# A two-layer trunk on one NeuronCore: seven block products for a pair of up-projection tiles in place of eight

## The chip, the cores and the metric

The kernel runs on one core of a Trainium2 chip. The metric is the device time of one execution in microseconds (us), as the median of several runs. The engines are TensorE (PE in the profile, PEld for its weight loads), VectorE (DVE), ScalarE (ACT), GpSimd (POOL) and SyncE (SP, which issues the DMAs).

## The reference

The reference is a trunk of two layers on 512 tokens of width 1024, with 16 learned meta tokens ahead, 528 in all. The first layer's mixer is a sparse attention over selected keys, the second's a differential attention. Each layer ends with a gated ConvFFN, and the change is in these two ConvFFNs:

```python
def conv_ffn(h, w_up, conv_w, conv_b, w_down):
    Tp = h.shape[1]
    u = h @ w_up                                   # 1024 -> 2 * 2816
    up = jnp.pad(u, ((0, 0), (CONV_W - 1, 0), (0, 0)))
    c = conv_b + sum(up[:, j:j + Tp] * conv_w[j] for j in range(CONV_W))
    gate, val = jnp.split(c, 2, axis=-1)
    return (jax.nn.silu(gate) * val) @ w_down      # 2816 -> 1024
...
    h = h + conv_ffn(rms_norm(h, ln_ffn_g[i]), w_up[i], conv_w[i], conv_b[i], w_down[i])
```

Everything is float32.

## The kernel before

Activations lie transposed: features on the partitions, tokens on the free axis. The state `h` is 8 tiles of 128 features by 528 tokens. For a matmul each float32 operand is split into a high part in fp32r (a cast on ScalarE) and a low part (the difference, on VectorE or GpSimd), and a product is the sum of three matmuls: high by high, high by low, low by high. A matmul has one weight block of 128 by 128 and moves the columns of one half of the tokens (272 and 256 in the first layer; 260 and 256 in the second, which leaves out 12 meta tokens; down-projections of the second move 512 at once).

The weights go through `Weights`: a DMA on SP brings a tile of up to 8 blocks of K by 128 outputs into `raw` (512 KB, three buffers), `split` makes `hi` and `lo` (L111, L113; three buffers each), `take` gives the next pair to TensorE, `done` frees it, and `pump` loads and splits as far as buffers are free, in the order in which the tiles were planned.

A ConvFFN (`ffn`, L1050) normalises `h` and then walks over f = 0 to 21. For each f it computes two up tiles, gate (e = 0) and value (e = 1), in `lin` (L227): 8 blocks of K, two halves of the tokens, three matmuls each, 48 matmuls into a PSUM tile of two banks. `evac` (L1061) applies the convolution: a ScalarE pass with scale and bias (L1065) and two VectorE instructions that add the shifted columns (L1068), all reading PSUM. After the value tile ScalarE takes SiLU (L1073), VectorE the product (L1074), and the activation is split into `ah` and `al` (L1077, L1078). After f = 6, 12, 17 and at the end, `down` (L1120) multiplies the 6, 6, 5 and 5 activations gathered since with the down weights: 8 output tiles one after the other, and VectorE adds each from PSUM to `h` (L1116).

PSUM has eight banks: two tiles of two banks (tag `sp`: up tiles and every other down tile) and four single ones (tag `one`). Instructions are traced in the program's order; the framework then orders each engine's queue by priorities and a time model, and sets the semaphores.

Of the kernel before, what the change touches and what calls it, by code (L numbers as in the profile page):

```python
# [9 lines left out]
F32 = mybir.dt.float32  # L10
# [4 lines left out]
DRAM = bass.MemoryType.DRAM  # L15

# [50 lines left out]
class Weights:  # L67
# [4 lines left out]
    RAW = 3  # L72
    RING = 3

    def __init__(self, nc, pool, par):
        self.nc, self.pool, self.par = nc, pool, par
        self.units, self.loads, self.raw, self.out = [], [], {}, {}
        self.loaded = self.scaled = self.ready = self.taken = self.freed = 0
        self.held = 0

    def add(self, src, n=8, m=128, g=None, lo="v", fold=None):
        self.units.append((n, m, lo))
        self.loads.append((src, n, m, g, fold))

    def load(self):
        src, n, m, g, fold = self.loads[self.loaded]
        raw = self.pool.tile([128, 8, 128], F32, tag="raw", name="raw", bufs=self.RAW)
        dst = raw[:, :n, :m]
        self.nc.sync.dma_start(dst if fold is None else dst.rearrange("p (a k) c -> p a k c", a=fold), src)
        self.raw[self.loaded] = raw  # L90
        self.loaded += 1

    def scale(self):
        src, n, m, g, fold = self.loads[self.scaled]
        if g is not None:
            r = self.raw[self.scaled][:, :n, :m]
            self.nc.gpsimd.tensor_tensor(r, r, self.par[:, g:g + n, None].to_broadcast([128, n, m]), op=OP.mult)  # L97
        self.scaled += 1

    def split(self):  # L100
        nc = self.nc
        n, m, lo = self.units[self.ready]
        raw = self.raw.pop(self.ready)
        self.freed += 1
        r = raw[:, :n, :m]
        hi = self.pool.tile([128, 8, 128], F32R, tag="hi", name="hi", bufs=self.RING)
        lt = self.pool.tile([128, 8, 128], F32R, tag="lo", name="lo", bufs=self.RING)
        if lo == "pp":
            nc.gpsimd.tensor_scalar(hi[:, :n, :m], r, 1.0, 1.0, op0=OP.mult, op1=OP.mult)
        else:  # L110
            nc.scalar.copy(hi[:, :n, :m], r)  # L111
        eng = nc.vector if lo == "v" else nc.gpsimd
        eng.tensor_tensor(lt[:, :n, :m], r, hi[:, :n, :m].bitcast(F32), op=OP.subtract)  # L113
        self.out[self.ready] = (hi, lt)
        self.held += 1
        self.ready += 1

    def can_split(self):
        return self.ready < self.scaled and self.held < self.RING

    def pump(self, stop=None):
        while stop is None or self.ready < stop:
            if self.loaded < min(len(self.loads), self.freed + self.RAW):
                self.load()
            elif self.scaled < self.loaded:
                self.scale()
            elif self.can_split():
                self.split()
            else:
                return  # L130
# [10 lines left out]
    def done(self):  # L141
        self.held -= 1
# [7 lines left out]
class Trunk:  # L150
# [88 lines left out]

    def halves(self, name):  # L240
# [11 lines left out]
    def setup(self):  # L252
# [15 lines left out]
        self.wt = Weights(nc, self.W, par)  # L268
# [62 lines left out]
    PARTS = ((0, 6), (6, 12), (12, 17), (17, 22))  # L331
    PW = ((0,0),(0,1),(1,0))

    def plan_ffn(self, l):
        wu, wd = self.a["w_up"][l], self.a["w_down"][l]
        for f in range(NF):
# [1311 lines left out]
```

## Time and profile before

| | us |
|---|---|
| Median of 3 runs | 1387.37 |
| Lowest and highest run | 1386.98, 1393.93 |
| The profiled execution, its own time | 1384.77 |
| Its span, first to last instruction | 1383.0 |

The page gives each engine's busy time, the chain of waits that ended last, and the costliest groups of instructions; a matmul's recorded duration is longer than its share of the stream, since matmuls are pipelined, so the rate is read from the distance of events that repeat. In the trace the tiles of f = 0 and 1 of the first ConvFFN are computed around 280 to 306 us.

### The profile page before, as it was taken

What the parts mean: (1) busy time and instruction counts of PE and PEld (TensorE: products, weight loads), DVE (VectorE), ACT (ScalarE), POOL (GpSimd) and SP (SyncE); (2) the same over time, 40 slices, a digit from 0 to 9 for tenths busy, and PEclk for the clock granted to TensorE, in tenths of its full rate; (3) what the DMA queues carried; (4) which work ended last, traced back from release to release, by engine and by line L of the source; (5) the groups of instructions that cost most, each with busy time, mean ns of one, the idle gap of its engine ahead of it and who ended that gap; (6) DMA issues with size and microseconds to landing.
All of it is one profiled execution on the core that took longest, in us unless ns stands there. A gap on an engine that the chain in (4) does not pass through costs nothing.

```text
span 1383.0 us, 25034 instructions
## 1 busy us (share of the span) xinstructions
PE 1324.3 (96%) x10072; PEld 1278.4 (92%) x10072; DVE 852.2 (62%) x1734; ACT 589.3 (43%) x1114; POOL 286.2 (21%) x334
## 2 busy tenths in 40 slices
PE   5999899999999999999799999989899999999998
PEld 4999789899999999999799999989799899899897
DVE  6499977665445445555756767775755445545453
ACT  4453555554224333234435555655544234333231
POOL 3514533400000000002554533444500000000000
PEclk9999989999999999999999989999999999999999
DMA  7412222122332232323223222212222332332422
GB/s 233 118 48 89 84 70 80 61 78 81 88 95 82 85 107 69 106 83 89 73 80 85 79 66 64 72 48 69 77 62 84 93 109 85 88 107 64 121 71 97
DMA packets 46995, 118.98 MB, mean 86 GB/s; under 512 B 5936, under 2 KB 15456, under 8 KB 46880
## 3 DMA queue, kind: packets, MB, share of 16 engines
q1 hardware_dynamic: 46128, 114.57, 27.8%
q0 software_dynamic: 752, 2.82, 0.7%
q8 instruction: 79, 1.29, 0.4%
q14 instruction: 36, 0.29, 0.1%
HBM read 112.46 MB, written 4.91 MB: 85 GB/s over the span
## 4 chain that ended last, share of the span: by engine, by line
PE 84%; DVE 8%; ACT 2%; issue 2%; POOL 2%; DMA 1%; SPq 0%; POOLq 0%; DVEq 0%; ACTq 0%
PE lin L222 56%; PE dn L1105 17%; PE pv L1005 1%; PE stq L567 1%; PE pv L1453 1%; DVE lo L113 1%; PE sa L910 1%; DVE acc L447 1%; ACT hi L111 1%; PE linh L222 1%; DVE xl L517 1%; PE pt L1014 1%; PE stk L557 1%; PE pt L1467 1%; PE sb L1379 1%
## 5 line engine op out<-in xcount | busy, mean ns | idle before, releaser
L222 PE MATMUL lin<-xh,hi 128*128 128x256 f32 (+3 forms) x2208 | 635.0, 289 | 12.7 <-DVE ht L434 7.0
L222 PE MATMUL lin<-xl,hi 128*128 128x256 f32 (+3 forms) x2208 | 634.1, 287 | 2.4 <-POOL xl L517 1.8
L222 PE MATMUL lin<-xh,lo 128*128 128x256 f32 (+3 forms) x2208 | 634.5, 288 | 0.0
L222 PEld LDWEIGHTS lin<-xh,hi 128*128 128x128 f32 (+1 forms) x2208 | 420.6, 191 | 16.3 <-ACT xh L542 5.0
L222 PEld LDWEIGHTS lin<-xl,hi 128*128 128x128 f32 (+1 forms) x2208 | 421.5, 191 | 4.3 <-POOL xl L517 2.2
L222 PEld LDWEIGHTS lin<-xh,lo 128*128 128x128 f32 (+1 forms) x2208 | 421.6, 191 | 0.1
L111 ACT CAST hi<-raw 128x1024 fp32r<-128x1024 f32 (+3 forms) x209 | 199.4, 956 | 332.3 <-PE lin L222 167.0
L113 DVE TENSOR_TENSOR lo<-raw,hi 128x1024 fp32r<-128x1024 f32 (+3 forms) x180 | 201.9, 1123 | 223.1 <-ACT hi L111 222.7
L1105 PE MATMUL dn<-ah,hi 128*128 128x256 f32 (+2 forms) x528 | 142.3, 322 | 0.5 <-DVE ht L1116 0.5
L1105 PE MATMUL dn<-al,hi 128*128 128x256 f32 (+2 forms) x528 | 142.5, 321 | 0.0
L1105 PE MATMUL dn<-ah,lo 128*128 128x256 f32 (+2 forms) x528 | 141.9, 321 | 0.0
L1068 DVE SCALAR_TENSOR_TENSOR c<-lin,par,c 128x512 f32<-128x512 f32 (+2 forms) x172 | 129.7, 755 | 2.9
L1116 DVE TENSOR_TENSOR ht<-dn,ht 128x256 f32<-128x256 f32 (+2 forms) x96 | 46.6, 514 | 116.3 <-PE dn L1105 116.3
L1105 PEld LDWEIGHTS dn<-ah,hi 128*128 128x128 f32 x528 | 88.9, 188 | 9.0 <-DVE ht L1116 0.8
L1105 PEld LDWEIGHTS dn<-ah,lo 128*128 128x128 f32 x528 | 88.9, 188 | 7.8
L1105 PEld LDWEIGHTS dn<-al,hi 128*128 128x128 f32 x528 | 89.0, 188 | 7.4
L447 POOL TENSOR_TENSOR acc<-acc,nsq 128x256 f32<-128x256 f32 (+2 forms) x18 | 16.6, 929 | 378.2 <-PE dn L1105 360.7
L113 POOL TENSOR_TENSOR lo<-raw,hi 128x1024 fp32r<-128x1024 f32 (+1 forms) x31 | 70.3, 2268 | 64.7 <-ACT hi L111 64.3
L1077 ACT CAST ah<-c 128x528 fp32r<-128x528 f32 (+1 forms) x44 | 27.6, 627 | 102.9 <-DVE c L1074 102.9
L1065 ACT ACTIVATE c<-lin,par 128x528 f32<-128x528 f32 (+1 forms) x86 | 67.2, 781 | 0.0
L1073 ACT ACTIVATE c<-c 128x528 f32<-128x528 f32 (+1 forms) x44 | 28.1, 639 | 83.7 <-DVE c L1068 83.7
L97 POOL TENSOR_TENSOR raw<-raw,par 128x1024 f32<-128x1024 f32 x24 | 47.3, 1971 | 69.1 <-DMA raw<-w_kv 34.7
(255 smaller groups left out, 1760.8 us busy)
## 6 DMA issues: line engine op xcount, KB each, us to landing
raw<-w_up SPq DMA_DIRECT2D x88, 512.0 KB, 3.5
raw<-w_down SPq DMA_DIRECT2D x32, 384.0 KB, 3.1
raw<-w_down SPq DMA_DIRECT2D x32, 320.0 KB, 2.9
raw<-w_in SPq DMA_DIRECT2D x16, 512.0 KB, 3.6
raw<-w_kv SPq DMA_DIRECT2D x16, 512.0 KB, 3.7
nb<-nbias SPq DMA_DIRECT2D x16, 264.0 KB, 2.7
raw<-w_o_a SPq DMA_DIRECT2D x8, 512.0 KB, 3.6
raw<-w_q SPq DMA_DIRECT2D x8, 512.0 KB, 3.5
```

The costliest lines, as they stand in the source:

```text
L97: self.nc.gpsimd.tensor_tensor(r, r, self.par[:, g:g + n, None].to_broadcast([128, n, m]), op=OP.mult)
L111: nc.scalar.copy(hi[:, :n, :m], r)
L113: eng.tensor_tensor(lt[:, :n, :m], r, hi[:, :n, :m].bitcast(F32), op=OP.subtract)
L222: i = self.nc.tensor.matmul(o, w[wi][:, kw + k, :m], x[s][xi][:, kx + k, c0:HN[s]], start=(first and p == 0), stop=(last and p == 2))
L447: eng.tensor_tensor(acc, acc, sq[:, :n], op=OP.add)
L517: i = eng.tensor_tensor(xl[:, m, o:o + n], xfs[m][:, :n], xh[:, m, o:o + n].bitcast(F32), op=OP.subtract)
L1065: nc.scalar.activation(t[:, :n], u[:, off + t0:off + T], AF.Identity, bias=b, scale=w2)
L1068: nc.vector.scalar_tensor_tensor(t[:, z:n], u[:, off + t0 + z - d:off + T - d], w, t[:, z:n], op0=OP.mult, op1=OP.add)
L1073: nc.scalar.activation(c[:, :n], c[:, :n], AF.Silu)
L1077: nc.scalar.copy(ah[:, :n], c[:, :n])
L1105: nc.tensor.matmul(part(t, c0, c1, o), w[wi][:, k, :], acts[f][ai][:, c0:c1], start=(first and p == 0), stop=(last and p == 2))
L1116: nc.vector.tensor_tensor(hv, part(t, c0, c1, o), hv, op=OP.add)
```

## The change

For f = 2 to 21 the gate and the value tile of one f are computed together in `up_pair`. The two tiles are taken as a 2 by 2 block matrix: G1, G2 are the gate's blocks of K 0 to 3 and 4 to 7, V1, V2 the value's. The tokens are halved at the middle (264 columns each in the first layer, 258 in the second). In place of 8 block products of 12 matmuls there are 7 (`product`), a scheme of Strassen's kind:

- weight sums S1 = V1 + V2, S2 = S1 - G1, S3 = G1 - V1, S4 = G2 - S2, four VectorE adds of 4 x 128 columns for each pair (`sum`), which are then split like other weights;
- token sums T, once per ConvFFN (`input_sums`): TensorE adds the blocks in PSUM by matmuls with the identity and minus the identity, and ScalarE and VectorE split them; these steps stand between those of the tiles of f = 0 and 1;
- the products accumulate in PSUM in the two-bank tiles `g` and `v`; ScalarE copies the first product from `g` to `v` and the second to SBUF (`p5`), and VectorE adds twice from `v` and `p5` into `g` and `v`.

Per pair the streams hold: in `wt` the gate tile, S12 and S34 (8 blocks each), in a second `Weights` object `ws` with half-size buffers the value's second half (4 blocks) and the down weights. The down groups are now 4, 4, 4, 4 and 6. The first four are computed inside later pairs, one tile per slot: pairs f = 4 to 19 hold a late tile each, f = 5 to 20 a middle one, each in two halves (of 12 matmuls in the first layer, 6 of 512 columns in the second), and VectorE adds it to `h`. The last group (16 to 21) is computed behind the pairs as before.

Over the pairs the queues of TensorE, VectorE and ScalarE hold the program's order (`manual_schedule`); `early` places a cast and `late` the low part by hand, and the pump only loads. The product, the split of the activation and the late tile's add of pair f stand at the start of pair f + 1.

The diff, cut to its core:

```diff
...
+    def sum(self):
+        p, half = divmod(self.summed, 2)
+        g, v = self.pairs[p]
+        kind = ("S12", "S34")[half]
+        assert g["ok"] and v["ok"] and kind not in self.sums, "no weights to sum up"
+        t = self.extra.tile([128, 8, 128], F32, tag=kind, name=kind, bufs=1)
+        gw, vw = g["raw"], v["raw"]
+        add = self.nc.vector.tensor_tensor
+        if half == 0:
+            add(t[:, 0:4], vw[:, 0:4], vw[:, 4:8], op=OP.add)
+            add(t[:, 4:8], t[:, 0:4], gw[:, 0:4], op=OP.subtract)
+            self.s2 = t[:, 4:8]
+        else:
+            add(t[:, 4:8], gw[:, 4:8], self.s2, op=OP.subtract)
+            add(t[:, 0:4], gw[:, 0:4], vw[:, 0:4], op=OP.subtract)
+        for r in (g, v):
...
+        self.sums[kind] = t
+        self.summed += 1
+        self.pump()
...
+    def cast(self):
+        nc = self.nc
+        kind, r, k, n, m, lo = self.units[self.ready + len(self.half)]
+        src = r["raw"] if kind == "raw" else self.sums.pop(kind)
+        src = src[:, k:k + n, :m]
...
+            nc.scalar.copy(hi[:, :n, :m], src)
+        self.half.append((hi, lt, src))
+    def rest(self):
...
+        eng.tensor_tensor(lt[:, :n, :m], src, hi[:, :n, :m].bitcast(F32), op=OP.subtract)
+        if kind == "raw":
+            r["reads"] -= 1
...
-    PARTS = ((0, 6), (6, 12), (12, 17), (17, 22))
-    PW = ((0,0),(0,1),(1,0))
+    PLAIN = 2
+    PARTS = ((0, 4), (4, 8), (8, 12), (12, 16))
+    TAIL = 16
+    PW = ((0, 0), (0, 1), (1, 0))
+    def down_slots(self):
+        late = {f1 + q: (p, 2 * q) for p, (_, f1) in enumerate(self.PARTS) for q in range(4)}
+        return late, {f + 1: (p, m + 1) for f, (p, m) in late.items()}
     def plan_ffn(self, l):
...
-                self.wt.add(wu[f + NF * e], lo=('p' if (f, e) in self.PW else 'v'))
-            for f0, f1 in self.PARTS:
-                if f == (f1 if f1 < NF else NF - 1):
-                    for m in range(KC):
-                        self.wt.add(wd[m][:, f0:f1, :], n=f1 - f0, lo="vv"[m % 2])
+                wt.add(wu[f + NF * e], lo='p' if (f, e) in self.PW else 'v')
+        for f in range(self.PLAIN, NF):
+            g, v = (wt.load_of(wu[f + NF * e]) for e in range(2))
+            wt.unit("raw", g)
+            pair = wt.pair(g, v)
+            wt.unit("S12", pair)
+            wt.unit("S34", pair)
+            for slot in (mid, late):
+                if f in slot:
+                    p, m = slot[f]
+                    f0, f1 = self.PARTS[p]
+                    ws.add(wd[m][:, f0:f1, :], n=4)
+            ws.unit("raw", v, 4, 4)
+        ws.ends.append(len(ws.loads))
+        for m in range(KC):
+            wt.add(wd[m][:, self.TAIL:NF, :], n=NF - self.TAIL, lo="v")
...
+            def input_sums():
...
+                def add(t, k, blocks, first):
+                    for p, (z, b) in enumerate(blocks):
+                        xs, k0, c = B[b]
+                        for e in range(2):
+                            nc.tensor.matmul(t, same[z], xs[2 + e][:, k0 + k, c:c + N],
+                                             start=(first and p == 0 and e == 0), stop=(p == len(blocks) - 1 and e == 1),
+                                             skip_group_check=not first)
+                    self.pe(2 * len(blocks) * mm_cost(N))
+                def split(t, j, k, sign):
+                    hi, lo = (TT[j][z][:, k, :N] for z in range(2))
+                    nc.scalar.mul(hi, t, sign)
+                    if sign > 0:
+                        nc.vector.tensor_tensor(lo, t, hi.bitcast(F32), op=OP.subtract)
+                    else:
+                        nc.vector.scalar_tensor_tensor(lo, t, sign, hi.bitcast(F32), op0=OP.mult, op1=OP.subtract)
...
+                    t = bank()
+                    add(t, k, ((0, (1, 2)), (1, (1, 1))), True)
+                    split(t, 0, k, 1.0)
+                def three(k):
+                    banks[k] = bank()
+                    add(banks[k], k, ((0, (2, 2)), (1, (1, 2))), True)
+                    split(banks[k], 2, k, 1.0)
+                def two(k):
+                    add(banks[k], k, ((0, (1, 1)),), False)
+                    split(banks[k], 1, k, 1.0)
+                def four(k):
+                    add(banks[k], k, ((1, (2, 1)),), False)
+                    split(banks[k], 3, k, -1.0)
+                for fn, k in ((three, 0), (one, 0), (two, 0), (one, 1), (four, 0), (three, 1), (one, 2), (two, 1),
+                              (one, 3), (four, 1), (three, 2), (three, 3), (two, 2), (two, 3), (four, 2), (four, 3)):
+                    fn(k)
+                    yield
+            def product(out, w, wk, xs, xk, c0, first=True):
+                for k in range(4):
+                    for p, (wi, xi) in enumerate(((0, 0), (0, 1), (1, 0))):
+                        nc.tensor.matmul(out, w[wi][:, wk + k, :], xs[xi][:, xk + k, c0:c0 + N],
+                                         start=(first and k == 0 and p == 0), stop=(k == 3 and p == 2), skip_group_check=not first)
+                    self.pe(3 * mm_cost(N))
+                    self.poll()
+            def up_pair(f):
...
+                more = f + 1 < NF
+                n3, ns = wt.taken, ws.taken
+                a, b = ((z.get(f) and down(*z[f])) or iter(()) for z in (at_mid, at_late))
+                g = ps.tile([128, 1024], F32, tag="sp", name="g")
+                g0, g1 = g[:, off + st0:512], g[:, 512:512 + N]
+                for i in range(ns, ns + (f in at_mid) + (f in at_late) + 1):
+                    ws.early(i)
+                before = rest.pop(f - 1, iter(()))
+                next(before, None)
+                while ws.half:
+                    ws.late()
+                G, S12 = wt.take(), wt.take()
+                product(g0, G, 0, x0, 0, st0)
+                v = ps.tile([128, 1024], F32, tag="sp", name="v")
+                v0, v1 = v[:, off + st0:512], v[:, 512:512 + N]
+                nc.scalar.copy(v0, g0)
+                next(before, None)
+                product(g1, S12, 0, TT[0], 0, 0)
+                p5 = fp.tile([128, 264], F32, tag="p", name="p5", bufs=2)[:, :N]
+                nc.scalar.copy(p5, g1)
+                if more:
+                    wt.sum()
+                next(a, None)
+                product(v0, S12, 4, TT[1], 0, 0, False)
+                nc.vector.tensor_tensor(g1, v0, p5, op=OP.add)
+                if more:
+                    wt.sum()
+                product(g0, G, 4, x0, 4, st0, False)
+                wt.done()
+                wt.done()
+                wt.early(n3 + 3)
+                wt.late()
+                wt.early(n3 + 4)
+                next(a, None)
+                next(a, None)
+                if f in at_mid:
+                    ws.done()
+                if f + 1 in at_mid:
+                    ws.early(ws.taken + (f in at_late) + 1)
+                S34 = wt.take()
+                product(v0, S34, 0, TT[2], 0, 0, False)
+                nc.vector.tensor_tensor(v1, v0, p5, op=OP.add)
+                wt.late()
+                ws.late()
+                product(g1, S34, 4, x1, 4, mid - 264, False)
+                wt.done()
+                convolve(g, f, 0, off)
+                wt.early(n3 + 5)
+                wt.late()
+                next(b, None)
+                nc.scalar.activation(conv[0][:, :n], conv[0][:, :n], AF.Silu)
+                A22 = ws.take()
+                product(v0, A22, 0, TT[3], 0, 0, False)
+                convolve(v, f, 1, off)
+                next(b, None)
+                if f in at_late:
+                    ws.done()
+                ws.done()
+                rest[f] = finish_pair(f, conv[0], conv[1], b)
+            def finish_pair(f, c, t, b):
+                nc.vector.tensor_tensor(c[:, :n], c[:, :n], t[:, :n], op=OP.mult)
+                next(b, None)
+                yield
+                split_acts(f, c)
+                yield
...
-            self.run(self.lin_many(x, first[2:], 0))
+            more = input_sums()
+            self.run(self.beside(self.lin_many(x, first[2:], 0), more))
...
+            def down(p, m):
+                f0, f1 = self.PARTS[p]
+                t, w = new(), ws.take()
+                for k in range(f1 - f0):
+                    if k == (f1 - f0) // 2:
+                        yield
+                    block(t, w, f0 + k, k, cols, k == 0, k == f1 - f0 - 1)
+                yield
+                add(t, m, cols, False)
+                yield
...
-            for f in range(1, NF):
+            at_late, at_mid = self.down_slots()
+            with self.tc.issue_after(self.low.ins):
+                wt.sum()
+                wt.sum()
+            for f in range(1, self.PLAIN):
                 for e in range(2):
                     if (f, e) != (1, 0):
-                        self.run(self.lin(x, lambda u, f=f, e=e: evac(u, f, e), start=st0, tag="sp"))
-                for f0, f1 in self.PARTS[:-1]:
-                    if f == f1:
-                        down(f0, f1)
+                        self.run(self.beside(self.lin(x, lambda u, f=f, e=e: evac(u, f, e), start=st0, tag="sp"), more))
+            self.run(more)
+            wt.auto = ws.auto = False
+            with self.tc.manual_schedule(engines=ENGINES):
+                for f in range(self.PLAIN, NF):
+                    up_pair(f)
+                for _ in rest.pop(NF - 1):
+                    pass
+            wt.auto = ws.auto = True
+            wt.pump()
             if l == 0:
                 self.table(AF.Sqrt, conv[0][:, 0:1])
-            down(*self.PARTS[-1])
+            down_last(self.TAIL, NF)
```

## Rows read from the trace of the kernel before

**Rows 1.** Page part 1: busy us (share of the span) xinstructions of each engine.

```profile
...
PE 1324.3 (96%) x10072; PEld 1278.4 (92%) x10072; DVE 852.2 (62%) x1734; ACT 589.3 (43%) x1114; POOL 286.2 (21%) x334
...
```

**Rows 2.** Page part 4, the chain that ended last: share of the span by line.

```profile
...
PE lin L222 56%; PE dn L1105 17%; PE pv L1005 1%; PE stq L567 1%; PE pv L1453 1%; DVE lo L113 1%; PE sa L910 1%; DVE acc L447 1%; ACT hi L111 1%; PE linh L222 1%; DVE xl L517 1%; PE pt L1014 1%; PE stk L557 1%; PE pt L1467 1%; PE sb L1379 1%
...
```

**Rows 3.** Timeline of ScalarE, both ConvFFNs: start us, us, engine, instruction, idle before, releaser.

```profile
...
300.14 0.79 ACT L1065 ACTIVATE c<-lin,par 128x528 f32<-128x528 f32 x1
...
306.02 0.79 ACT L1065 ACTIVATE c<-lin,par 128x528 f32<-128x528 f32 x1
...
1131.45 0.78 ACT L1065 ACTIVATE c<-lin,par 128x512 f32<-128x512 f32 x1
...
1137.15 0.78 ACT L1065 ACTIVATE c<-lin,par 128x512 f32<-128x512 f32 x1
...
```

**Rows 4.** Timeline of VectorE in down-projections of both ConvFFNs.

```profile
...
485.84 0.77 DVE L1116 TENSOR_TENSOR ht<-dn,ht 128x256 f32<-128x256 f32 x2 [2.83 <-PE dn L1105]
...
494.65 0.77 DVE L1116 TENSOR_TENSOR ht<-dn,ht 128x256 f32<-128x256 f32 x2 [2.35 <-PE dn L1105]
...
1094.11 0.69 DVE L1116 TENSOR_TENSOR ht<-dn,ht 128x512 f32<-128x512 f32 x1 [1.56 <-PE dn L1105]
...
1098.29 0.69 DVE L1116 TENSOR_TENSOR ht<-dn,ht 128x512 f32<-128x512 f32 x1 [2.54 <-PE dn L1105]
...
```

**Rows 5.** Lines by form: line, engine, instruction xcount, busy us, mean ns, idle before.

```profile
...
L111 ACT CAST hi<-raw 128x1024 fp32r<-128x1024 f32 x136 | 142.4, 1047 | 193.6 <-PE lin L222 129.7 <-PE dn L1105 56.1 <-POOL tm L889 2.8
...
L1065 ACT ACTIVATE c<-lin,par 128x528 f32<-128x528 f32 x43 | 33.9, 787 | 0.0
...
L1116 DVE TENSOR_TENSOR ht<-dn,ht 128x512 f32<-128x512 f32 x32 | 22.0, 690 | 60.2 <-PE dn L1105 60.2
...
L1074 DVE TENSOR_TENSOR c<-c,c 128x528 f32<-128x528 f32 x22 | 15.6, 708 | 0.7
...
L1116 DVE TENSOR_TENSOR ht<-dn,ht 128x272 f32<-128x272 f32 x32 | 13.7, 430 | 0.0
...
```

**Rows 6.** Timeline of VectorE at the opening of the first ConvFFN.

```profile
...
289.31 1.23 DVE L113 TENSOR_TENSOR lo<-raw,hi 128x1024 fp32r<-128x1024 f32 x1 [5.98 <-ACT hi L111]
...
290.45 0.76 DVE L1068 SCALAR_TENSOR_TENSOR c<-lin,par,c 128x527 f32<-128x527 f32 x1
...
307.29 1.56 DVE L1068 SCALAR_TENSOR_TENSOR c<-lin,par,c 128x527 f32<-128x527 f32 x2
...
```

**Rows 7.** Timeline of all engines, opening of the first ConvFFN.

```profile
...
291.17 0.29 PE L222 MATMUL linh<-xh,hi 128*128 128x272 f32 x1
...
292.57 0.38 ACT L1092 COPY u<-linh 128x272 f32<-128x272 f32 x1
...
293.17 0.36 PE L222 MATMUL lin<-xh,hi 128*128 128x272 f32 x1 [1.46 <-DVE c L1068]
...
```

**Rows 8.** Windows: stretch, us, busy us of each engine, PEclk, DMA share, GB/s.

```profile
...
293.00:305.00 12.00, 11.83 (x97) 11.86 (x98) 9.08 (x13) 6.31 (x8) 0.00 (x0) 1.00 0.49 150
...
305.00:317.00 12.00, 12.00 (x101) 12.00 (x100) 6.94 (x9) 4.95 (x7) 0.00 (x0) 1.00 0.28 89
...
475.00:513.00 38.00, 38.00 (x313) 38.00 (x312) 14.88 (x23) 9.77 (x11) 0.00 (x0) 1.00 0.36 108
...
286.00:294.00 8.00, 6.54 (x53) 6.35 (x52) 4.69 (x6) 5.70 (x8) 0.00 (x0) 1.00 0.26 70
...
661.00:668.00 7.00, 3.35 (x24) 2.83 (x22) 6.68 (x10) 3.75 (x7) 2.01 (x2) 1.00 0.21 73
...
668.00:675.00 7.00, 6.06 (x29) 5.37 (x30) 6.89 (x15) 2.62 (x7) 3.94 (x3) 0.51 0.45 143
...
```

**Rows 9.** Page part 6, DMA issues: KB each, median us from issue to landing.

```profile
...
raw<-w_up SPq DMA_DIRECT2D x88, 512.0 KB, 3.5
...
```

**Rows 10.** Waits of VectorE: us in total, times, longest us.

```profile
...
DVE al L1078 <- ACT ah L1077: 26.8, 38, 0.8
...
```

More of the change, by code (lines that the diff above doesn't have):

```diff
@@ L67, with __init__ @@
 class Weights:
[L72 to L79, printed above, removed]
-    def add(self, src, n=8, m=128, g=None, lo="v", fold=None):
-        self.units.append((n, m, lo))
-        self.loads.append((src, n, m, g, fold))
-    def load(self):
[L86 to L90, printed above, removed]
+    def __init__(self, nc, pool, par, depth=8, tag="", ring=3):
+        self.nc, self.pool, self.par, self.depth, self.tag, self.ring = nc, pool, par, depth, tag, ring
+        self.loads, self.units, self.pairs, self.out, self.sums = [], [], [], {}, {}
+        self.loaded = self.scaled = self.summed = self.ready = self.taken = self.finished = 0
+        self.extra, self.peer, self.ends, self.end = None, None, [], 1 << 30
+        self.auto, self.half = True, []
@@ new lines, in load_of, with unit, pair @@
+    def load_of(self, src, n=8, m=128, g=None, fold=None):
+        d = {"src": src, "n": n, "m": m, "g": g, "fold": fold, "reads": 0, "raw": None, "ok": False}
+        self.loads.append(d)
+        return d
+    def unit(self, kind, r, k=0, n=8, m=128, lo="v"):
+        if kind == "raw":
+            r["reads"] += 1
+        self.units.append((kind, r, k, n, m, lo))
+    def pair(self, g, v):
+        self.pairs.append((g, v))
+        for r in (g, v):
+            r["reads"] += 2
+        return len(self.pairs) - 1
@@ new lines, in rest, with early @@
+    def rest(self):
+        hi, lt, src = self.half.pop(0)
+        kind, r, k, n, m, lo = self.units[self.ready]
+        eng = self.nc.vector if lo == "v" else self.nc.gpsimd
+        eng.tensor_tensor(lt[:, :n, :m], src, hi[:, :n, :m].bitcast(F32), op=OP.subtract)
+        if kind == "raw":
+            r["reads"] -= 1
+        self.out[self.ready] = (hi, lt)
+        self.ready += 1
+        self.pump()
+    def split(self):
+        self.cast()
+        self.rest()
+    def early(self, i):
+        if i != self.ready + len(self.half) or i >= len(self.units):
+            return
+        kind, r = self.units[i][:2]
+        assert i < self.ring or i - self.ring < self.finished, "no place"
+        assert r["ok"] if kind == "raw" else kind in self.sums, "no weights"
+        self.cast()
@@ L121, in pump, with late, step @@
+    def late(self):
+        if self.half:
+            self.rest()
+    def step(self):
+        if self.can_load():
+            self.load()
+        elif self.scaled < self.loaded:
+            self.scale()
+        elif self.auto and self.can_split():
+            self.split()
+        else:
+            return False
+        return True
     def pump(self, stop=None):
         while stop is None or self.ready < stop:
[L123 to L129, printed above, removed]
+            if not self.step() and not (stop is None and self.peer is not None and self.peer.step()):
@@ L141, in done @@
     def done(self):
-        self.held -= 1
+        self.finished += 1
         self.pump()
@@ L238, in lin, with beside @@
             self.wt.done()
+    @staticmethod
+    def beside(main, more):
+        for _ in main:
+            yield
+            next(more, None)
     def halves(self, name):
@@ L520, in low @@
                     chain(i)
+                    self.low = i
             last = [None]
```

129 lines of the change are left out of this document (82 added, 47 removed).

## The prediction

> **What bounds the kernel now.** I read the page's busy shares first. TensorE is busy for 96% of the span, VectorE for 62% [rows 1], so only fewer columns through TensorE, or fewer pauses, can shorten it. The chain of waits says where: the up-projections and other full tiles (`lin`) hold 56% of the span, the down-projections (`dn`) 17% [rows 2].
>
> The rate comes from the timelines. In the first ConvFFN two neighbouring tiles of 48 matmuls are released 5.88 us apart, 0.1225 us a matmul of 264 columns on average; in the second 5.70 us, 0.1188 us for 258 [rows 3]. Down tiles are as steady: two tiles of 36 matmuls in 8.81 us (0.1224 each), and one of 18 matmuls of 512 columns in 4.18 us (0.232) [rows 4]. Between these TensorE doesn't pause: in the stretches 305-317 and 475-513 it is busy all the time at a granted clock of 1.00 (2.4 GHz), while VectorE works for 58% and 39% [rows 8].
>
> **What is removed from TensorE.** A pair of up tiles (gate and value) is two output blocks by two halves of K by two halves of the tokens: 8 block products of 12 matmuls. From f = 2 on there are 7. Twenty pairs in each of two layers lose 12 matmuls: 20 x 12 x 0.1225 = 29.4 us in the first, 20 x 12 x 0.1188 = 28.5 us in the second, 57.9 us together. The down-projection keeps all its matmuls (22 blocks of K by 8 tiles, grouped 4, 4, 4, 4, 6 in place of 6, 6, 5, 5).
>
> **What is added to TensorE.** The four token sums T are made by matmuls with plus and minus the identity: 4 steps of k with 4 + 4 + 2 + 2 matmuls, 48 a layer of half width: 48 x 0.1225 + 48 x 0.1188 = 11.6 us. Net of both: 46.3 us less.
>
> **What is added beside TensorE.** Now VectorE has to keep up. An instruction of it starts some 0.08 us before the recorded end of the one before (289.31 + 1.23 against 290.45, [rows 6]), so back to back it costs its duration less 0.08. A full pair of the first layer (with two down tiles, f = 5 to 19) puts on VectorE: 3 low parts of whole tiles at 1.15 (before: 2); 7 instructions on 512 columns at 0.61 (3 low parts of half tiles and the 4 weight sums; the nearest row is 0.69 for 512 columns); 2 Strassen adds and 4 down adds of 264 columns at 0.35 (0.43 in its row); 2 convolutions at 1.48 (two dependent instructions take 1.56); product and low part of the activation at 0.63 each [rows 5, 6]. Sum: 3.45 + 4.27 + 2.10 + 2.96 + 1.26 = 14.0 us. TensorE has 84 + 48 matmuls, 16.2 us. In the second layer it is 13.8 us against 84 x 0.1188 + 24 x 0.232 = 15.6 us. ScalarE has some 8 us: 3 whole and 3 half casts, 2 copies, 2 convolution passes, 2 passes on the activation, by the rows of the cast (1.05 for 1024 columns) and the pass (0.79) less 0.08 each [rows 5, 7]. So in full pairs TensorE stays the bound by 2 us. In a pair without down tiles (f = 2, 3, 21) VectorE has 14.0 - 2 x (0.61 + 0.70) = 11.4 us and TensorE 84 x 0.1225 = 10.3 us: there VectorE is the bound by 1.1 us.
>
> No row of before shows an add that reads one PSUM bank and writes another, or a ScalarE copy from PSUM into PSUM. Nearest are the down add (0.43 us from PSUM for 272 columns) and the copy of 272 columns (0.38 us) [rows 5, 7]. From below: as these, back to back, 0.35 and 0.30; from above: twice as long, which puts 0.9 us on VectorE in a pair and still leaves 1.2 us. Neither can gain. I take the row.
>
> **The waits of the fixed order.** Inside a pair four accesses to PSUM follow one another with TensorE, and for each I ask what covers it. Third product after the copy into v0: the copy ends 0.17 + 0.38 us after the first product's share of the stream (a matmul is recorded with 0.29 us at a spacing of 0.12 [rows 3, 7]), and the second product covers it with 1.47. Fifth after the first add: 0.17 + 0.43 + 0.05, covered by the fourth. Seventh after the second add: the same, covered by the sixth. First product of the next pair after the gate's convolution has read `g`: 0.17 + 0.79 + 1.56 + 0.09 = 2.6 us (the last terms, 0.05 and 0.04, are my estimate of a semaphore's way), covered by the seventh product and, in pairs with a late down tile, by its two halves: 4.4 us. Without one only 1.5 us cover it, and TensorE stops for 1.1 us: after pairs 2, 3, 20 and 21, 4.4 us a layer. Behind VectorE's two adds stand the next pair's sums and low parts, and behind those the gate's convolution; in a full pair this queue has the 2 us to spare.
>
> **Opening and end.** Pair 2 needs the sums T. Their 32 splits (16 on ScalarE, 16 on VectorE at 0.35 = 5.6 us), 4 weight sums (2.4 us), and low parts of S34 and of a half tile (1.8 us) come on top of what VectorE does for f = 0 and 1: 9.8 us. It idles there 2.9 us in 293-305 and 5.1 us in 305-317 [rows 8]: some 2 us late. Already before, TensorE stood 1.46 us in this place for VectorE [rows 7]; that stays. The 1.1 us that VectorE is behind in each of pairs 2, 3 and 21 fall partly into the stops just counted; I take half, 1.7 us. With 4.4 that is 8.1 us a layer, 16 us in all. Bounds: nothing, if the stops hide one another; 30 us, if all add up and the T splits stop TensorE as well (16 x 0.43 us a layer).
>
> **Loads.** A full pair reads 2 x 512 KB and 2 x 256 KB in 16.2 us, 97 GB/s; 475-513 moved 108 [rows 8]. The next but one value tile is issued when the gate tile is freed after the fourth product, at least 10 us before its first sum; a tile lands in 3.5 us [rows 9]. SP's order holds nothing of this up. I price it at nothing; if that cover fails, each pair waits for a landing, up to 3.5 us.
>
> **Sum.** The profiled execution took 1384.8 us (span 1383.0). 1384.8 - 57.9 + 11.6 + 16 = 1354.5. The median of the runs is 2.6 us above that execution, so about 1357.
>
> **Rivals.**
> 1. VectorE's pace cancels the gain. If its 22 instructions (20 in the second layer) don't overlap, a pair costs 14.0 + 22 x 0.08 = 15.8 us (15.4); the low part of the activation waits 0.70 us for ScalarE on the mean (26.8 us in 38 [rows 10]). One such wait a pair makes 16.5 and 16.1 us, 0.3 and 0.5 over the matmuls, 20 x 0.8 = 16 us back, 1373; two make 1401; midway 1387. For it: 22 instructions with waits in an order that can't be rearranged. Against: 2 us of reserve, and back-to-back starts are what dense stretches show.
> 2. Slower: lock-step. VectorE reaches both adds and both convolutions before their products or ScalarE's pass (0.79 us [rows 5]) are done, stands 0.79 us at each of the four, and TensorE then waits at the next pair's first product. 14.0 + 4 x 0.79 = 17.2 us, 1.0 over TensorE's 16.2: 40 x 1.0 more, 1397. It decides from 16.2 + 30 / 40 = 16.9 us a pair on. For it: each wait heads VectorE's queue and the next waits stand behind. Against: before each add stand 1.2 us of weight sums that need nothing of TensorE, so it should arrive late rather than early.
> 3. The stops vanish: opening and end hide in each other, 1341 to 1346.
> 4. The clock falls. The half clock in 668-675 (0.51) followed a stretch in which TensorE was busy for 3.35 of 7 us; the pause of 1.46 us in 286-294 left it at 1.00 [rows 8]. The worst pairs here pause about as in the second. If the four stops a layer that I counted led to it at two of them, each 7 us at half clock as in that row, 4 x 3.5 us come on top and more waits behind them: 1371 to 1377. The Trainium skill has a rule for this ("TensorE: Matmul & The Clock Gate", section "A second HAM failure mode: psum-queue depth-cycling"): frequent short idling between groups of matmuls that cycle through PSUM makes the clock swing between its levels. The trace of before agrees only for long pauses; by that rule the time is this rival's.
>
> That the products stay at 8 is no rival: the matmuls can be counted in the code.
>
> **How the numbers follow.** Forecast 0.57 (1349 to 1366), rival 1 0.17, rival 2 0.14, rival 3 0.08, rival 4 0.04. About 0.5% (7 us) is what a measurement can tell from no change. Rival 1 is spread evenly over 1373 to 1401, and so divides into 0.05 faster by more than that, 0.08 within it and 0.04 slower. Faster: 0.57 + 0.08 + 0.04 + 0.05 = 0.74; within: 0.08; slower: 0.14 + 0.04 = 0.18. The range 1343 to 1392 leaves out rival 2, the upper third of rival 1 and the lower end of rival 3, about 0.2.
>
> **What would show it.** Right: full pairs of 16.2 and 15.6 us with TensorE busy throughout at a clock of 1.00; pauses of about a microsecond before the first product after pairs 2, 3, 20 and 21, released by the gate's convolution; VectorE busy near 85% in the pairs; 84 up matmuls a pair in place of 96, and 48 for T a layer. Wrong: full pairs longer than 16.9 us, pauses before the third, fifth or seventh product, low parts released by a DMA, or a clock of 0.5 inside the pairs.

## The result and the profile after

The changed kernel takes 1424.17 us (median of 4 runs, 1422.17 to 1425.05) against 1387.17 us for the kernel before in the same comparison (1385.75 to 1393.93). The ratio is 1.0255 with a 95% interval of 1.022 to 1.029: slower by about 37 us, where 1357 was forecast. The profiled execution took 1424.05 us.

The page, against [rows 1]: the span, and busy us (share) and instructions of each engine.

```profile
...
span 1422.2 us, 24955 instructions
...
PE 1303.1 (92%) x9688; PEld 1238.2 (87%) x9688; DVE 1076.8 (76%) x2126; ACT 689.8 (49%) x1330; POOL 286.8 (20%) x334
...
```

The 384 fewer matmuls are the forecast's 480 less 96, but the busy time of TensorE fell by only 21 us, and its share from 96% to 92%. So its idle time doubled, from 59 to 119 us of the span; the last section says where the rest of the forecast's 46 us went. The chain still runs mostly on TensorE, now through `g`, `v` and `dn` (against [rows 2]):

```profile
...
PE lin L306 20%; PE g L1240 17%; PE dn L1374 17%; PE v L1240 12%; DVE c L1331 2%; PE pv L1742 1%; PE stq L681 1%; DVE g L1279 1%; DVE lo L176 1%; PE pv L1119 1%; ACT v L1270 1%; PE linh L306 1%; DVE acc L560 1%; ACT hi L168 1%; DVE xl L630 1%
...
```

Neither of these says what is wrong; the waits do. TensorE's waits after: who waited for whom, us in total, times, longest us.

```profile
...
PE g L1240 <- ACT v L1270: 27.4, 40, 1.7
PE g L1240 <- DVE g L1279: 24.1, 40, 0.8
...
PE g L1240 <- DVE c L1331: 6.6, 6, 1.1
...
PE T L1198 <- DVE Tl L1207: 3.6, 2, 1.9
...
```

Two lines stand there 40 times each, once in every pair of both layers, and neither is in the forecast. The third line is in it (8 times 1.1 us were expected), and so is the fourth, in the bounds. The timeline of TensorE in one full pair shows where the two stand (start us, us, engine, line, instruction, idle before and releaser):

```profile
...
404.46 0.28 PE L1240 MATMUL g<-xh,lo 128*128 128x264 f32 x1
405.24 0.39 PE L1240 MATMUL g<-Th,hi 128*128 128x264 f32 x1 [0.50 <-ACT v L1270]
405.46 0.29 PE L1240 MATMUL g<-Tl,hi 128*128 128x264 f32 x1
405.59 0.28 PE L1240 MATMUL g<-Th,lo 128*128 128x264 f32 x1
...
409.60 0.28 PE L1240 MATMUL v<-Th,lo 128*128 128x264 f32 x1
410.48 0.39 PE L1240 MATMUL g<-xh,hi 128*128 128x264 f32 x1 [0.60 <-DVE g L1279]
410.70 0.28 PE L1240 MATMUL g<-xl,hi 128*128 128x264 f32 x1
...
```

404.46 is the last matmul of the first product, into `g0`. The next one, the first of the second product, goes into `g1`, the other bank of `g`; it needs nothing that the copy makes. Still it starts 0.78 us later in place of 0.12, released by ScalarE's copy out of `g0` (L1270). 410.48 is the first of the fourth product, into `g0`; it waits for VectorE's first add, which writes `g1` (L1279), and starts 0.88 us after the one before. Each first matmul after a stop is followed at 0.22 us in place of 0.12. A full pair so loses 0.66 + 0.10 + 0.76 + 0.10 = 1.62 us, and 40 pairs at that price 65 us (an estimate: 32 of them hold a middle tile as this one does), more than the 46.3 us that the matmuls save.

ScalarE's copy marks the pair; its timeline gives the period, in the first layer and in the second (against [rows 3]):

```profile
...
404.82 0.36 ACT L1270 COPY v<-g 128x264 f32<-128x264 f32 x1 [1.01 <-PE g L1240]
...
422.49 0.36 ACT L1270 COPY v<-g 128x264 f32<-128x264 f32 x1 [1.01 <-PE g L1240]
...
1202.03 0.36 ACT L1270 COPY v<-g 128x258 f32<-128x258 f32 x1 [0.97 <-PE g L1240]
...
1219.29 0.36 ACT L1270 COPY v<-g 128x258 f32<-128x258 f32 x1 [0.98 <-PE g L1240]
...
```

Full pairs take 17.67 and 17.26 us, against the 16.2 and 15.6 forecast: 1.47 and 1.66 more. The operations themselves cost what was expected. Lines by form (count, busy us, mean ns, idle before; against [rows 5]):

```profile
...
L142 DVE TENSOR_TENSOR S<-raw 128x512 f32<-128x512 f32 x40 | 28.5, 713 | 0.0
...
L1331 DVE SCALAR_TENSOR_TENSOR c<-g,par,c 128x527 f32<-128x527 f32 x20 | 15.3, 767 | 5.2 <-ACT c L1328 3.2
...
L1279 DVE TENSOR_TENSOR g<-v,p 128x264 f32<-128x264 f32 x20 | 8.8, 442 | 20.0 <-PE v L1240 20.0
...
L1270 ACT COPY v<-g 128x264 f32<-128x264 f32 x20 | 7.3, 363 | 21.3 <-PE g L1240 17.0 <-DVE c L1331 4.1
...
```

The two unseen operations, the add across banks (0.442 us) and the copy from PSUM into PSUM (0.363), lie near the rows taken for them (0.43 and 0.38). The windows (stretch, us, busy us of each engine, PEclk, DMA share, GB/s; against [rows 8]) show two full pairs and, below, the fall of the clock at the opening of each ConvFFN:

```profile
...
387.00:422.00 35.00, 32.80 (x263) 32.10 (x263) 28.53 (x44) 16.30 (x24) 0.00 (x0) 1.00 0.29 91
...
305.00:310.50 5.50, 4.88 (x24) 4.59 (x25) 3.64 (x8) 2.42 (x6) 0.00 (x0) 0.69 0.00 0
...
1051.00:1056.00 5.00, 3.14 (x15) 2.86 (x16) 4.65 (x11) 1.95 (x5) 0.00 (x0) 0.82 0.00 0
...
```

In the pairs TensorE is busy for 94% at full clock, VectorE for 82%. So the clock is out as a cause in the full pairs; what has to be told apart is whether the tile and the order hold TensorE, or VectorE's pace does.

### The profile page after: what moved, and what is told of

It is laid out like the page before. It is cut to its first block, busy times and chain, and to the rows that moved or that the text cites. A ratio compares the mean times of both kernels' runs of the same rounds, so it can differ in the third digit from the quotient of the medians.

```text
span 1422.2 us, 24955 instructions
## 1 busy us (share of the span) xinstructions
PE 1303.1 (92%) x9688; PEld 1238.2 (87%) x9688; DVE 1076.8 (76%) x2126; ACT 689.8 (49%) x1330; POOL 286.8 (20%) x334
## 4 chain that ended last, share of the span: by engine, by line
PE 77%; DVE 13%; ACT 5%; issue 3%; POOL 1%; DMA 1%; SPq 0%; ACTq 0%; DVEq 0%; POOLq 0%
PE lin L306 20%; PE g L1240 17%; PE dn L1374 17%; PE v L1240 12%; DVE c L1331 2%; PE pv L1742 1%; PE stq L681 1%; DVE g L1279 1%; DVE lo L176 1%; PE pv L1119 1%; ACT v L1270 1%; PE linh L306 1%; DVE acc L560 1%; ACT hi L168 1%; DVE xl L630 1%
## 5 line engine op out<-in xcount | busy, mean ns | idle before, releaser
L306 PE MATMUL lin<-xh,hi 128*128 128x256 f32 (+3 forms) x928 | 271.9, 298 | 13.0 <-DVE ht L547 6.4
L306 PE MATMUL lin<-xl,hi 128*128 128x256 f32 (+3 forms) x928 | 272.0, 294 | 3.3 <-DVE xl L630 1.7
L306 PE MATMUL lin<-xh,lo 128*128 128x256 f32 (+3 forms) x928 | 271.6, 294 | 0.0
L176 DVE TENSOR_TENSOR lo<-raw,hi 128x512 fp32r<-128x512 f32 (+3 forms) x196 | 177.8, 922 | 21.0 <-ACT hi L168 18.1
L306 PEld LDWEIGHTS lin<-xh,hi 128*128 128x128 f32 (+1 forms) x928 | 179.1, 195 | 16.7 <-ACT xh L656 8.5
L306 PEld LDWEIGHTS lin<-xl,hi 128*128 128x128 f32 (+1 forms) x928 | 180.9, 195 | 5.0 <-DVE xl L630 3.1
L306 PEld LDWEIGHTS lin<-xh,lo 128*128 128x128 f32 (+1 forms) x928 | 180.9, 195 | 0.0
L1240 PE MATMUL g<-xh,hi 128*128 128x264 f32 (+1 forms) x480 | 140.7, 293 | 30.8 <-DVE g L1279 24.1
L1240 PE MATMUL v<-Th,lo 128*128 128x264 f32 (+1 forms) x480 | 136.3, 284 | 0.0
L1240 PE MATMUL v<-Tl,hi 128*128 128x264 f32 (+1 forms) x480 | 136.2, 284 | 0.0
```

The source lines that it names most:

```text
L176: eng.tensor_tensor(lt[:, :n, :m], src, hi[:, :n, :m].bitcast(F32), op=OP.subtract)
L306: i = self.nc.tensor.matmul(o, w[wi][:, kw + k, :m], x[s][xi][:, kx + k, c0:HN[s]], start=(first and p == 0), stop=(last and p == 2))
L1240: nc.tensor.matmul(out, w[wi][:, wk + k, :], xs[xi][:, xk + k, c0:c0 + N], start=(first and k == 0 and p == 0), stop=(k == 3 and p == 2), ...
```

## The experiments

**Theory A**: the waits come from the two-bank tile. The program's waits know `g` as one object, so an access to one bank holds up the next access to the other, and nothing stands between to cover it. **Theory B**: VectorE and ScalarE reach their work late in the fixed order, and moving the two accesses only moves the wait.

The runs below belong to two other comparisons, in which the kernel before took 1386.02 us (e1 to e4) and 1386.5 us (e5 to e8), against 1387.17 above. Differences to the changed kernel are between medians of different comparisons. Full pairs are given as two periods, the first layer's and the second's.

**e1_copy_late**: the copy is issued behind the second product.

```
-                nc.scalar.copy(v0, g0)
-                next(before, None)
                 product(g1, S12, 0, TT[0], 0, 0)
+                nc.scalar.copy(v0, g0)
+                next(before, None)
```

> Only the copy of the first product (g to v, ScalarE) is placed behind the second product in the program. Theory A (a matmul into one bank of the two-bank tile g waits for the access to its other bank that stands before it in the program): the pause of 0.66 us before the second product, and the 0.1 us behind it, go in the 32 full or middle pairs, where half a down tile covers the later copy: 32 x 0.76 = 24 us less, about 1400 us. Theory B (VectorE's queue sets the pair, and TensorE's pauses are only where that shows): the pause moves to another place and the time stays at 1420 to 1425.

Measured: 1389.32 us (1385.71 to 1395.86), ratio to the kernel before 1.0032 [1.0011, 1.0054], so 35 us less than the changed kernel. Full pairs 16.91 and 16.5 us, 0.76 less, which is the first stop of the timeline above. TensorE's waits:

```profile
...
PE g L1240 <- DVE g L1279: 27.1, 40, 1.4
...
PE g L1240 <- DVE c L1331: 6.6, 6, 1.1
...
PE v L1240 <- ACT v L1271: 4.5, 8, 0.8
...
PE T L1198 <- DVE Tl L1207: 0.7, 2, 0.4
...
```

The line for the copy is gone from the second product; the one for the add stays. A smaller one appears 8 times, in the pairs without a middle down tile, where only the second product now lies between the end of the first and the third, which needs the copy. From the first product of f = 2 to the last of f = 21 the two layers together are 34.1 us shorter in the traces: 24 us come from the 32 pairs with a middle tile, 6 together from the first pairs of the two layers, where the wait for T is shorter too (the last line, against 3.6 us) and the clock doesn't fall, and 4 from the other six pairs. In pairs 3 and 4 only some 0.4 us each is gained, although the second product had waited 1.7 us there: now the third product waits 0.5, and the fourth 1.3 to 1.4 in place of 0.6. Why the wait for T is shorter was not taken apart.

**e2_add_late**: the first add is issued behind the fourth product.

```
-                nc.vector.tensor_tensor(g1, v0, p5, op=OP.add)
                 if more:
                     wt.sum()
                 product(g0, G, 4, x0, 4, st0, False)
+                nc.vector.tensor_tensor(g1, v0, p5, op=OP.add)
```

> Only VectorE's first add into g is placed behind the fourth product in the program. Theory A: the pause of 0.76 us before the fourth product, and the 0.1 us behind it, go in the 32 pairs in which half a down tile stands between the fourth and the fifth product: 32 x 0.86 = 27.5 us less, about 1397 us. Theory B: the add only comes later in a full queue, 1420 to 1430.

Measured: 1395.1 us (1392.32 to 1396.49), ratio 1.0074 [1.0051, 1.0096], 29 us less than the changed kernel. Full pairs 16.81 and 16.39, 0.86 less: the second stop. The waits are the mirror image:

```profile
...
PE g L1240 <- ACT v L1270: 29.7, 40, 1.8
...
PE v L1240 <- DVE g L1282: 4.7, 8, 0.6
...
```

**e3_both_late**: both edits.

> Both of these edits together. Theory A: the two gains add up, 52 us less, about 1372 us, with full pairs of 16.2 us in the first layer and 15.6 in the second. Theory B: a pair can't fall below VectorE's own pace; with 17 us a pair, 1400 or more.

Measured: 1363.59 us (1360.62 to 1367.48), ratio 0.985 [0.982, 0.988]: 1.5% faster than before. ScalarE's copies give the periods, 16.10 and 15.63 us:

```profile
...
415.13 0.36 ACT L1271 COPY v<-g 128x264 f32<-128x264 f32 x1 [2.50 <-PE g L1240]
...
431.23 0.36 ACT L1271 COPY v<-g 128x264 f32<-128x264 f32 x1 [2.49 <-PE g L1240]
...
1188.67 0.36 ACT L1271 COPY v<-g 128x258 f32<-128x258 f32 x1 [2.43 <-PE g L1240]
...
1204.30 0.36 ACT L1271 COPY v<-g 128x258 f32<-128x258 f32 x1 [2.43 <-PE g L1240]
...
```

The window over two full pairs (columns as above) and TensorE's waits:

```profile
...
372.00:404.15 32.15, 32.15 (x266) 32.15 (x266) 29.03 (x45) 16.06 (x25) 0.00 (x0) 1.00 0.33 99
...
```

```profile
...
PE v L1240 <- DVE g L1282: 7.1, 8, 1.3
...
PE g L1240 <- DVE c L1331: 6.6, 6, 1.1
...
PE v L1240 <- ACT v L1271: 4.9, 8, 1.2
...
PE T L1198 <- DVE Tl L1207: 2.2, 4, 1.0
...
```

TensorE is busy for all of 32.15 us, with VectorE busy for 90% of them beside it. Theory B is refuted as the cause: with the same work on VectorE, at its higher density, the pair runs at TensorE's rate.

**e7_own_bank**: the changed kernel's order, but the second product goes into a bank that is a tile of its own (`q`); `p5` is copied from there. This kernel leaves out the matmuls that open the accumulation in `g1`: the second half of S34 now accumulates there behind VectorE's add alone. Its sums in `g1` are not the block's, so it serves for its time alone; the number and the sizes of the instructions are the same.

```
-                product(g1, S12, 0, TT[0], 0, 0)
+                q = ps.tile([128, 512], F32, tag="one", name="q")[:, :N]
+                product(q, S12, 0, TT[0], 0, 0)
...
-                nc.scalar.copy(p5, g1)
+                nc.scalar.copy(p5, q)
```

> The changed kernel with one difference: the second product goes into a PSUM tile of its own (one bank), from which ScalarE copies it, and the order of the program stays. Theory A (the wait comes from the two-bank tile that the second product shares with the first one's copy): the pause before the second product goes in all pairs, 24 to 35 us less, 1389 to 1400 us; the pause before the fourth product stays. Theory B (the copy as such, or ScalarE's queue, holds TensorE at this place): no change, 1420 to 1425. The columns that the fourth weight sum's product accumulates onto may hold old data at the edge; the work is the same.

Measured: 1387.59 us (1382.96 to 1388.88), ratio 0.9997 [0.9976, 1.0019], 37 us less than the changed kernel. Full pairs 16.91 to 16.98 and 16.49. The waits:

```profile
...
PE g L1240 <- DVE g L1280: 28.0, 40, 1.6
...
PE v L1240 <- ACT v L1270: 1.2, 6, 0.3
...
```

In both kernels the second product writes another bank than the one that the copy reads. Only the tile differs, and with it the second product's 40 waits on the copy go. The add's, where the tile is still shared, stay. So the first wait belongs to the tile and not to the bank. For the second wait this was not tried by itself with a tile of its own; e2 shows only that the order decides it.

**e4_mid_between**: copy and add stay where the change put them, and the two halves of the middle down tile move to where the stops are, one behind the first product and one behind the third.

```
                 nc.scalar.copy(v0, g0)
                 next(before, None)
+                next(a, None)
                 product(g1, S12, 0, TT[0], 0, 0)
...
-                next(a, None)
                 product(v0, S12, 4, TT[1], 0, 0, False)
                 nc.vector.tensor_tensor(g1, v0, p5, op=OP.add)
                 if more:
                     wt.sum()
+                next(a, None)
                 product(g0, G, 4, x0, 4, st0, False)
...
-                next(a, None)
```

> The order of copy and add is as in the changed kernel; instead the two halves of the middle down tile stand between the first and the second product and between the third and the fourth. Theory A: the same two waits are now covered by 1.46 us of other matmuls each, 32 x 1.62 = 52 us less, 1372 us, or up to 8 us more if the add now comes late to the fifth product. Theory B: 1400 or more.

Measured: 1367.82 us (1365.15 to 1369.56), ratio 0.9877 [0.9854, 0.9901], full pairs 16.05 and 15.63. The waits:

```profile
...
PE g L1240 <- ACT v L1270: 11.6, 8, 1.9
...
PE g L1240 <- DVE g L1279: 4.7, 8, 0.6
...
```

Both lines fall from 40 to 8, which are the pairs without a middle tile. The waits are still in the program; matmuls of another tile cover them. So they cost only where TensorE has nothing else to do.

**e8_more_vector**: e3 with the last two weight sums of each pair made twice, 1.2 us more on VectorE. This measures what is left of its reserve, by itself.

```
-            add(t[:, 4:8], gw[:, 4:8], self.s2, op=OP.subtract)
-            add(t[:, 0:4], gw[:, 0:4], vw[:, 0:4], op=OP.subtract)
+            for _ in range(2):
+                add(t[:, 4:8], gw[:, 4:8], self.s2, op=OP.subtract)
+                add(t[:, 0:4], gw[:, 0:4], vw[:, 0:4], op=OP.subtract)
```

> The kernel with copy and add behind, and VectorE makes the second two weight sums of each pair twice (1.2 us more a pair, the same values). If VectorE has the 2 us of reserve that the forecast gave it in a full pair (16.2 against 14.0), full pairs stay at 16.05 and 15.63 us and only the 8 pairs without a full load of down tiles get longer: 5 to 10 us more, 1369 to 1374 us. If VectorE sets the pace of all pairs, 38 x 1.2 = 46 us more, about 1409 us.

Measured: 1387.95 us (1384.88 to 1399.7), ratio 1.0013 [0.9983, 1.0043], 24 us more than e3: between the two expectations. ScalarE's copies and TensorE's waits:

```profile
...
406.65 0.36 ACT L1272 COPY v<-g 128x264 f32<-128x264 f32 x1 [2.50 <-PE g L1241]
...
423.15 0.36 ACT L1272 COPY v<-g 128x264 f32<-128x264 f32 x1 [2.50 <-PE g L1241]
...
1194.05 0.36 ACT L1272 COPY v<-g 128x258 f32<-128x258 f32 x1 [2.41 <-PE g L1241]
...
1210.26 0.36 ACT L1272 COPY v<-g 128x258 f32<-128x258 f32 x1 [2.43 <-PE g L1241]
...
```

```profile
...
PE v L1241 <- DVE g L1283: 18.5, 32, 2.5
...
```

The pairs are 16.50 and 16.21 us, and TensorE now waits for VectorE's first add 32 times in place of 8. Taking off the two added instructions (2 x 0.61, from the forecast's back-to-back duration of a 512-column instruction), I estimate that VectorE alone would need 15.28 and 14.99 us a pair. Against 16.05 and 15.63 that is a reserve of some 0.77 and 0.64 us. Two of VectorE's idle times in a pair of the first layer, 0.32 and 0.24 us, are waits for ScalarE:

```profile
...
403.16 1.57 DVE L1332 SCALAR_TENSOR_TENSOR c<-v,par,c 128x527 f32<-128x527 f32 x2 [0.32 <-ACT c L1329]
...
407.60 0.71 DVE L1339 TENSOR_TENSOR al<-c,ah 128x528 fp32r<-128x528 f32 x1 [0.24 <-ACT ah L1338]
...
```

**e5_plain4**: e3 with the pairs starting at f = 4 (two pairs less a layer), to give the opening more time.

```
-    PLAIN = 2
+    PLAIN = 4
...
-            with self.tc.issue_after(self.low.ins):
-                wt.sum()
-                wt.sum()
...
+                if f == self.PLAIN - 1:
+                    with self.tc.issue_after(self.low.ins):
+                        wt.sum()
+                        wt.sum()
```

> Copy and add as in the kernel with both behind, and the pairs begin at f = 4 in place of 2 (f = 2 and 3 are plain tiles; the first weight sums move to f = 3). There the two pairs took 31.9 us in the first layer from the start of the first product of f = 2 to that of f = 4, T matmuls included; two plain pairs take 23.5 us and the 27 T matmuls among them 3.3. If the opening is late because VectorE is (theory A), these 5 us a layer come back: 10 us less, about 1354 us. If the opening only moves to the first pair with a down tile (theory B), the pauses of 3 to 5 us a layer reappear at f = 4 and the 24 matmuls of 0.12 us that a layer now has more are a loss: 1364 to 1372.

Measured: 1358.66 us (1355.78 to 1363.29), ratio 0.9806 [0.9772, 0.984]: the lowest median of all versions, 2% under the kernel before. TensorE's waits:

```profile
...
PE v L1240 <- ACT v L1271: 5.8, 4, 2.4
...
PE g L1240 <- DVE c L1331: 2.2, 2, 1.1
...
```

Pairs 2 and 3 have no down tiles, so theirs were the bare waits. Two pairs a layer save no matmuls any more (4 x 12 x 0.12 = 5.8 us), and the median doesn't rise for it. The gain on e3 is 5 us of an expected 10, and the two intervals still touch, so a difference between e3 and e5 is not shown. The first pair, now f = 4, still stops for 2.4 us, and in the first layer it takes 18.16 us from its first product to the next pair's, against 15.50 for the same pair in e3: this takes back half of the 5.5 us by which it starts earlier.

**e6_plain4_last21**: e5 with f = 21, a pair without down tiles, computed as two plain tiles.

```
-        for f in range(self.PLAIN, NF):
+        for f in range(self.PLAIN, self.LAST):
...
+        for f in range(self.LAST, NF):
+            for e in range(2):
+                wt.add(wu[f + NF * e])
```

> As the run with pairs from f = 4, and f = 21 too as two plain tiles: pairs only where down tiles stand in them. The pair of f = 21 has no down tile and showed pauses before its first and third product; a plain one takes 11.8 us against some 14.2 of distance. Theory A: 2 us a layer less than with f = 21 as a pair, about 1350 us. Theory B (the pauses move to the change-over): the same time as that run or up to 4 us more.

Measured: 1360.04 us (1358.51 to 1360.31), ratio 0.9809 [0.9781, 0.9838]: no gain over e5 and no loss is shown. The timelines of TensorE say why. First e5's, the first matmul of pair f = 21 and the first of the down tiles behind it; then e6's, the same for the two plain tiles:

```profile
...
600.79 0.36 PE L1240 MATMUL g<-xh,hi 128*128 128x264 f32 x1 [1.12 <-DVE c L1331]
...
613.17 0.40 PE L1374 MATMUL dn<-ah,lo 128*128 128x256 f32 x2
...
```

```profile
...
600.05 0.36 PE L306 MATMUL lin<-xh,hi 128*128 128x272 f32 x1 [1.12 <-DVE c L1335]
...
611.87 0.40 PE L1378 MATMUL dn<-ah,hi 128*128 128x256 f32 x2
...
```

The stop before the first product, 1.12 us, stands before the plain tiles too. Behind it the pair takes 12.38 us, of which 0.49 are four matmuls of the down tiles, and the plain tiles 11.82: only 0.1 us was to be had there, and 0.3 us in the second layer by the same reading, not the 2 us a layer of theory A.

## Why the prediction was wrong

**The step that failed is "The waits of the fixed order"**: "Inside a pair four accesses to PSUM follow one another with TensorE, and for each I ask what covers it." There are more, and two of those left out stop TensorE. I listed them by bank: the third product after the copy into `v0`, the fifth after the first add, the seventh after the second, and the next pair's first after the convolution. Two were not on the list because their banks differ: the second product after the copy out of `g0`, and the fourth after the add into `g1`. The program waits on the tile, and both its banks are one tile; e7 shows this for the first stop, and for the second it is argued from the same tile and from e2. The stops cost 0.76 + 0.86 = 1.62 us in a full pair, about 65 us in 40; e1 and e2 take them away one at a time (35 and 29 us) and e3 together (61 us). With that term the sum, 1354.5 + 65 = 1419.5, comes within 5 us of the execution's 1424.05. Part of that closeness is luck, as the end of this section shows.

A rule of the Trainium skill ("PSUM — Partial Sum Buffer", section "Summary: rules for kernel authors") says to aim a matmul at a different bank while PSUM is read, and to set the semaphore's guard by bank. This kernel did the first and waited all the same (0.50 us idle at 405.24), since its waits go by the tile; e7 shows that here the different bank had to be a different tile as well.

The trace of before held the pattern, and the prediction did not use it. The last group of down tiles in the first layer writes two passes into the two banks of one `dn` tile. TensorE's timeline of before:

```profile
...
661.30 0.29 PE L1105 MATMUL dn<-ah,lo 128*128 128x272 f32 x1
662.13 0.39 PE L1105 MATMUL dn<-ah,hi 128*128 128x272 f32 x1 [0.54 <-DVE ht L1116]
...
```

The second pass starts 0.83 us after the last matmul of the first, held by VectorE's add out of the other bank: the same kind of stop, at about the same price.

Point by point, the other steps:

- **Matmuls removed and added**: right. The count fell by 384, the distance is 0.122 us in the timeline, and pairs without the two stops take 16.05 to 16.10 and 15.63 us against 16.2 and 15.6 forecast.
- **Unseen operations**: right, 0.442 and 0.363 us. The 0.05 us that the waits hold for a semaphore's way is about right too: the matmul at 405.24 starts 0.06 us after the copy's end (404.82 + 0.36).
- **VectorE's reserve, 2 us in a full pair**: mis-sized. e8 leaves about 0.77 and 0.64 us. The durations were right (the sums 0.69 to 0.71 recorded, the convolution's two parts 0.77 each); what the sum of 14.0 us lacked is some 1.3 us between them. 0.56 of that are the two waits for ScalarE shown at e8, the kind that rival 1 named; the rest is in smaller gaps and was not taken apart. Rival 1's sum, 15.8 us, was too much the other way, and VectorE set no full pair's length as it stood.
- **Stops at the pairs without down tiles**: right in place and size for the convolution, after pairs 2, 3 and 20 (6 waits of 1.1 us). The forecast had 8, as it counted one after pair 21, behind which no pair stands. The 2 stops for T (3.6 us) are in the bounds.
- **Loads**: right at nothing; no wait of TensorE or VectorE after is put down to a transfer of weights. ScalarE waits for one once, 5.0 us behind the pairs of the second layer, where TensorE is busy throughout.
- **Rivals**: rival 2's sign came true and not its mechanism. It had TensorE waiting at the next pair's first product because VectorE stands idle; e8 and e3 show VectorE's pace inside TensorE's. Its price, 1.0 us a pair, was below the 1.62 found. Rival 4 holds for two moments only, behind the stops for T: a clock of 0.69 in 305 to 310.5 and of 0.82 in 1051 to 1056. The two stops in every full pair left the clock at 1.00 (387 to 422).
- **What would show it**: "full pairs longer than 16.9 us" was the sign that came. "Pauses before the third, fifth or seventh product" did not; they stand before the second and fourth.

With both waits out of the order the forecast's own sum is 6 us off: 1360.62 us for e3's profiled execution, for 1354.5. The eight pairs without a middle tile have 12.0 us of waits at the third and fifth product (7.1 + 4.9) that the sum doesn't hold; what makes up for the rest was not taken apart.

## What to carry to other kernels

For each access to a tile ask which instruction touches that tile next, whatever the bank or the columns, and what TensorE does in between: a tile of several banks is one object for the waits. Where both halves must be used in turn, issue the slow engine's access behind the next product, put other work between (e4), or give the halves tiles of their own (e7). Before pricing a new order, search the old trace for one place where the same pattern already stands and read its idle time.

## What the runs showed of the hardware

A stop of TensorE costs more than its recorded idle time. At 405.24 the profile books 0.50 us, but the matmul starts 0.66 us late against the steady distance, and the next one follows at 0.22 in place of 0.12: 0.76 us in all. At 410.48 it is 0.60 booked and 0.86 lost. The 51.5 us that the waits list for the two lines are so less than what the stops cost. The difference is booked as busy: with the same 9688 matmuls TensorE is busy for 1303.1 us in the changed kernel and for 1283.4 in e3, 20 us less, and 80 stops at 0.26 us make 21. This is why the busy time fell by only 21 us where 46 were taken out.

```profile
...
PE 1283.4 (94%) x9688; PEld 1231.7 (91%) x9688; DVE 1078.1 (79%) x2126; ACT 685.3 (50%) x1330; POOL 287.9 (21%) x334
...
```

An engine at 90% busy can still be covered in full: in e3 VectorE works 29.03 of 32.15 us in a fixed order, and the profile books no gap of TensorE. But 1.2 us more a pair cost 24 us in 40 pairs.
